# The SSD opening of a hybrid diffusion block: the positive part of the time steps on VectorE, the scan mask on GpSimd

## The chip, the cores and the metric

One core of a Trainium2 chip runs the whole program as one launch. The metric is device time in microseconds (us) of one execution. Of an engine's work the profile tells start and length of each instruction; the engines are TensorE (PE, with its weight loads as PEld), VectorE (DVE), ScalarE (ACT), GpSimd (POOL) and SyncE (SP), whose queue issues the DMAs. Each works through its own queue strictly in order and waits for the others by semaphores.

## The reference, cut to what matters

Two layers run over 512 latent tokens and 256 context tokens of width 1024. Layer 0 mixes tokens by attention, layer 1 by a bidirectional Mamba-2 state-space mixer (SSD); a gated feed-forward network with a short convolution follows each. What the edit touches is the front of the SSD mixer, in which a projection gives one time step for each token, head and direction:

```python
z, xbc, dt = jnp.split(h @ w_in, [D_INNER, D_INNER + CONV_DIM], axis=-1)
xbc = jax.nn.silu(dwconv_centred(xbc, conv_w, conv_b))
...
dt_f = jax.nn.softplus(dt_f.reshape(...) + dt_bias_f)
dt_b = jax.nn.softplus(dt_b.reshape(...) + dt_bias_b)
...
acs = jnp.cumsum(dtc * a, axis=2)          # within each chunk of 128 tokens
```

From `dt` and `acs` come all decays of the scan: `decay_end`, `chunk_decay`, and the matrix `exp(acs_q - acs_s)` of each chunk and head.

## The kernel before

Everything is float32. Each large matrix product is done as three matmuls on rounded halves (`mm3`, lines 108, 109 and 111: high weight by high activation, high by low, low by high), so every weight tile that SP loads (`wst`) is cast on ACT to its high half `wh` and split on DVE into its low half `wl` (lines 85 and 87). The buffers of these weight tiles rotate through ten places, so that the load, the cast and the split of a tile wait for a product some products earlier.

The program is written in the order of the mathematics; a scheduler of the framework then orders the instructions of each engine by a cost model of its own, so that an edit at one place can change the order at others. Buffers rotate by tags: of the PSUM tag `S` (two banks each, two of them) the projection tiles `ps_first` and `ps_in` take the slot that comes free first.

The SSD stage goes like this. `first_tiles` makes the first two products while the norm's last columns are still being worked out: `ps_dt`, the time steps (64 rows twice: rows 0 to 63 for tokens 0 to 383, rows 64 to 127 for tokens 384 to 767), and `ps_x0`, the first x tile; in the profile both are called `ps_first`. From `ps_dt` the time steps are made as softplus(v) = max(v, 0) + ln(1 + exp(-|v|)): `dte` holds |v| and its exponential, `dt` the positive part, `dtu`, `dtd` and `dtl` the logarithm with a correction; then `la` = dt times a (in `dte`), and `acs` by four scans on DVE (32 rows each, two directions, two halves), which multiply the running sum by a mask `msk` that is 0 at the first token of each chunk and 1 elsewhere.

Meanwhile `inproj(0)` makes the products of head group 0 in the order x, x, B, C, z, z. ACT copies each from PSUM to one of two buffers `raw`, multiplies by the middle tap (line 1063), DVE adds four taps (line 1065), ACT applies Silu (line 1069). When the first z tile is under way, `acs` and `dt` are transposed on TensorE (`ps_dtT`), copied to `acsT` and `dtT`, and `ps_end` spreads each chunk's last sum to all rows. Then `core(0)` makes decays, states and outputs of the group, interleaved with the products of the next; after eight groups the output projection (`ps_wo`, lines 1285 and later) multiplies the gated outputs `hhy`/`hly` (tiles 0 to 7) and `yh`/`yl` (8 to 15).

Of the kernel before, what the change touches and what calls it, by code (L numbers as in the profile page):

```python
# [7 lines left out]
P = 128  # L8
F32 = mybir.dt.float32
F32R = mybir.dt.float32r  # L10
AF = mybir.ActivationFunctionType
ALU = mybir.AluOpType
# [55 lines left out]
def t3(g, name, dt=F32, n=T):  # L68
    return g.t3p.tile([P, n], dt, tag="t3", bufs=g.n3, name=name)
# [148 lines left out]
def follow(g, bi):  # L218

    if g.last_act is not None:  # L220
        g.tc.add_manual_dep(bi.ins, g.last_act.ins.name, mybir.DependencyInfo(
            mybir.DependencyClass.NoSync, mybir.DependencyReason.DATA), reason="order of tables")
    g.last_act = bi
# [757 lines left out]
def ssd(g, x, norm, wf, bg, close):  # L981


    nc, I, tc = g.nc, g.I, g.tc
    par = lambda name, j, rows=P: g.par[:rows, PC[name] + j : PC[name] + j + 1]
# [13 lines left out]
    t2 = lambda nm, dt=F32, n=512: g.t3p.tile([P, n], dt, tag="t2", bufs=39, name=nm)  # L999
# [14 lines left out]
    TH = T // 2  # L1014
    r64 = lambda nm: t3(g, nm)[:, :TH]
    e, u, d0, dt = r64("dte"), r64("dtu"), r64("dtd"), r64("dt")
    for i in range(2):
        hs, src = slice(i * H2, (i + 1) * H2), ps[i * H2 : (i + 1) * H2, i * TH : (i + 1) * TH]
        nc.scalar.activation(e[hs], src, AF.Abs, bias=par("dtb", 0)[hs])
        nc.scalar.activation(dt[hs], src, AF.Relu, bias=par("dtb", 0)[hs])  # L1020
    follow(g, nc.scalar.activation(e, e, AF.Exp, scale=-1.0))

    nc.vector.tensor_scalar(u, e, 1.0, None, ALU.add)
# [6 lines left out]
    nc.vector.tensor_tensor(lnu, lnu, d0, ALU.add)  # L1030
    nc.vector.tensor_tensor(lnu, lnu, e, ALU.mult)
    nc.vector.tensor_tensor(dt, dt, lnu, ALU.add)
    la, acs, msk = e, r64("acs"), u
    nc.vector.tensor_scalar(la, dt, na, None, ALU.mult)
    nc.vector.memset(msk, 1.0)
    nc.vector.memset(msk.rearrange("p (c t) -> p c t", t=P)[:, :, 0:1], 0.0)

    for i in range(0, P, H2):
        f, b = slice(i, i + 32), slice(i + 32, i + 64)
# [185 lines left out]
    for gi in range(8):  # L1225
        i = -1
        for G in inproj(gi):
# [6 lines left out]
            if gi == 0 and i == 3:  # L1234
# [22 lines left out]
                for d in range(2):  # L1257
                    hs = slice(d * 32, d * 32 + 32)
# [4 lines left out]
                for d, t in enumerate((4, 5)):  # L1263
                    hs = slice(d * 32, d * 32 + 32)
# [92 lines left out]
def body(nc, tc, I, out, dbg=None):  # L1357
# [75 lines left out]
    def close():  # L1433
        phf.close()
        phx.close()

    x, nrm, first = ssd(g, x, nxt, wf, bg, close)
    phf = ExitStack()
    g.t3p, g.n3 = pool("pg", phf), 24
# [103 lines left out]
```

## Time and profile before

| | us |
|---|---|
| median of 3 runs | 1867.41 |
| lowest and highest | 1865.88 and 1868.11 |
| the profiled execution | 1865.96 |
| its span, first to last instruction | 1864.2 |
| PE busy | 1841.1 |
| DVE busy | 1305.0 |
| ACT busy | 809.6 |
| POOL busy | 304.3 |

The opening of the SSD stage lies at about 965 to 1010 us of the span, its output projection at about 1390 to 1490. In the rows of the timeline shown below stand start, length, engine, line, operation, what it writes and reads, and in brackets the idle time of the engine before it and what ended that.

### The profile page before, as it was taken

The numbers are of one execution on the slowest core, as the hardware profiler recorded it, in microseconds if no ns is written. First come the engines' busy times: TensorE is split into PE (matmuls) and PEld (weight loads), VectorE is DVE, ScalarE is ACT, GpSimd is POOL, SyncE is SP. The second block draws the span as 40 slices with busy tenths as digits, with TensorE's granted clock in tenths as the row PEclk, the third lists the DMA queues.
The fourth block names the chain that finished last, engine by engine and source line by source line (L and its number), as shares of the span: only waits on it lengthen the run. The fifth ranks groups of instructions, "written<-read, shape, count | busy, mean of one in ns | idle before, by whom it ended". The sixth has DMA issues, their size and how long they took to land.

```text
span 1864.2 us, 28839 instructions
## 1 busy us (share of the span) xinstructions
PE 1841.1 (99%) x11474; PEld 1542.8 (83%) x11474; DVE 1305.0 (70%) x1972; ACT 809.6 (43%) x1424; POOL 304.3 (16%) x266
## 2 busy tenths in 40 slices
PE   9999999999999999999999999999999999999999
PEld 8875655798888888888988888888888888888887
DVE  6588888778787776554487787777797575565655
ACT  4544434363222212222367667776666352323231
POOL 2123120040000000000032334444443210000000
PEclk9999999999999999999999999999999999999999
DMA  9233141124444552211224432433453223223232
GB/s 347 76 109 110 62 171 52 57 81 171 146 136 135 198 187 102 68 59 55 69 91 142 125 105 89 125 125 113 125 177 95 74 97 101 92 95 98 91 103 89
DMA packets 74070, 211.67 MB, mean 114 GB/s; under 512 B 9040, under 2 KB 14544, under 8 KB 73808
## 3 DMA queue, kind: packets, MB, share of 16 engines
q1 hardware_dynamic: 73936, 209.84, 34.2%
q8 instruction: 90, 1.47, 0.3%
q14 instruction: 44, 0.36, 0.1%
HBM read 198.79 MB, written 6.82 MB: 110 GB/s over the span
## 4 chain that ended last, share of the span: by engine, by line
PE 84%; DVE 7%; issue 3%; ACT 2%; POOL 2%; DMA 2%; SPq 0%; DVEq 0%; POOLq 0%; ACTq 0%
PE ps_up L111 10%; PE ps_up L109 10%; PE ps_up L108 10%; PE ps_d L108 7%; PE ps_d L109 6%; PE ps_d L111 6%; PE ps_in L111 4%; PE ps_in L109 4%; PE ps_in L108 4%; PE ps_s L700 2%; PE ps_o L664 2%; PE ps_st L1135 2%; PE ps_wo L111 1%; PE ps_wo L108 1%; PE ps_wo L109 1%
## 5 line engine op out<-in xcount | busy, mean ns | idle before, releaser
L87 DVE TENSOR_TENSOR wl<-wst,wh 128x1024 fp32r<-128x1024 f32 x207 | 258.0, 1246 | 221.4 <-PE ps_up L109 125.4
L85 ACT CAST wh<-wst 128x1024 fp32r<-128x1024 f32 x211 | 221.2, 1049 | 342.3 <-DMA wst<-in_wup 272.4
L111 PE MATMUL ps_up<-hhf,wl 128*128 128x512 f32 x1008 | 355.8, 353 | 0.0
L109 PE MATMUL ps_up<-hlf,wh 128*128 128x512 f32 x1008 | 355.8, 353 | 0.0
L108 PE MATMUL ps_up<-hhf,wh 128*128 128x512 f32 x1008 | 355.7, 353 | 0.0
L111 PEld LDWEIGHTS ps_up<-hhf,wl 128*128 128x128 f32 x1008 | 190.7, 189 | 25.9
L109 PEld LDWEIGHTS ps_up<-hlf,wh 128*128 128x128 f32 x1008 | 189.2, 188 | 25.9
L108 PEld LDWEIGHTS ps_up<-hhf,wh 128*128 128x128 f32 x1008 | 189.1, 188 | 25.8
L108 PE MATMUL ps_in<-hhs,wh 128*128 128x512 f32 (+1 forms) x560 | 203.7, 364 | 1.5 <-ACT dt L1020 1.5
L109 PE MATMUL ps_in<-hls,wh 128*128 128x512 f32 (+1 forms) x560 | 198.7, 355 | 0.0
L111 PE MATMUL ps_in<-hhs,wl 128*128 128x512 f32 (+1 forms) x560 | 198.2, 354 | 0.0
L108 PE MATMUL ps_d<-hdh,wh 128*128 128x512 f32 (+1 forms) x568 | 193.2, 342 | 0.3 <-ACT hdh L85 0.2
L109 PE MATMUL ps_d<-hdl,wh 128*128 128x512 f32 (+1 forms) x568 | 193.3, 341 | 0.0
L111 PE MATMUL ps_d<-hdh,wl 128*128 128x512 f32 (+1 forms) x568 | 193.1, 340 | 0.0
L877 DVE SCALAR_TENSOR_TENSOR X<-ps_d,mod,X 128x512 f32<-128x512 f32 (+1 forms) x224 | 125.1, 586 | 34.6 <-PE ps_d L111 34.0
L108 PEld LDWEIGHTS ps_in<-hhs,wh 128*128 128x128 f32 x560 | 105.5, 188 | 16.5 <-ACT dt L1020 1.7
L109 PEld LDWEIGHTS ps_d<-hdl,wh 128*128 128x128 f32 x568 | 106.9, 188 | 13.3 <-DVE hdl L87 0.4
L111 PEld LDWEIGHTS ps_d<-hdh,wl 128*128 128x128 f32 x568 | 107.6, 189 | 12.2
L111 PEld LDWEIGHTS ps_in<-hhs,wl 128*128 128x128 f32 x560 | 105.2, 188 | 14.8
L108 PEld LDWEIGHTS ps_d<-hdh,wh 128*128 128x128 f32 x568 | 106.4, 188 | 13.2 <-ACT hdh L85 0.7
L109 PEld LDWEIGHTS ps_in<-hls,wh 128*128 128x128 f32 x560 | 105.3, 188 | 13.4
L703 ACT ACTIVATE pr<-ps_s 128x1024 f32<-128x1024 f32 x56 | 57.2, 1022 | 104.6 <-PE ps_s L702 104.6
(339 smaller groups left out, 3661.2 us busy)
## 6 DMA issues: line engine op xcount, KB each, us to landing
wst<-in_wup SPq DMA_DIRECT2D x88, 512.0 KB, 3.3
wada<-in_adaT SPq DMA_DIRECT2D x56, 512.0 KB, 3.3
wst<-in_win SPq DMA_DIRECT2D x48, 512.0 KB, 3.4
wst<-in_wdown SPq DMA_DIRECT2D x44, 512.0 KB, 3.8
E<-ad SPq DMA_DIRECT2D x64, 256.0 KB, 6.4
wada<-in_adaB SPq DMA_DIRECT2D x24, 512.0 KB, 4.1
ec<-ead SPq DMA_DIRECT2D x64, 128.0 KB, 5.0
wst<-in_wout SPq DMA_DIRECT2D x16, 512.0 KB, 3.3
```

The costliest lines, as they stand in the source:

```text
L85: cast = keep(nc.scalar.copy(hi, src))
L87: keep(eng.tensor_tensor(lo, src, _r(hi), ALU.subtract))
L108: mm(out, wh, ah, start=first, stop=False)
L109: mm(out, wh, al, start=False, stop=False)
L111: mm(out, wl, ah, start=False, stop=last)
L664: nc.tensor.matmul(po[S64[e], :n], v, pr[:, 512 * e + off : 512 * e + off + n], start=first, stop=last)
L700: nc.tensor.matmul(outs[e], kk[e][a][S64[e], k], b[S64[e], q], start=i == 0, stop=False)
L703: exps.append(nc.scalar.activation(pr, ps, AF.Exp))
L877: nc.vector.scalar_tensor_tensor(ap, o[:, c0:c1], gate[:, m, v : v + 1], ap, ALU.mult, ALU.add)
L1135: nc.tensor.matmul(ps[:, d * 256 : (d + 1) * 256], Bt[:, t * P : (t + 1) * P], xw[d][t], start=t == ts[0], stop=t == ts[-1])
```

## The change

The Relu of each half, which ACT did behind the Abs of the same half, becomes one DVE instruction (add the bias, then maximum with 0) that reads the same half of `ps_dt` out of PSUM. The mask gets a buffer of its own from the tag `t2` (39 of them) instead of reusing `dtu`, and its two memsets move from DVE, between the steps of the logarithm, to POOL, with nothing ahead of them to wait for but their buffer.

```diff
@@ -1014,10 +1014,13 @@
     e, u, d0, dt = r64("dte"), r64("dtu"), r64("dtd"), r64("dt")
+    msk = t2("msk")[:, :TH]
+    nc.gpsimd.memset(msk, 1.0)
+    nc.gpsimd.memset(msk.rearrange("p (c t) -> p c t", t=P)[:, :, 0:1], 0.0)
     for i in range(2):
         hs, src = slice(i * H2, (i + 1) * H2), ps[i * H2 : (i + 1) * H2, i * TH : (i + 1) * TH]
         nc.scalar.activation(e[hs], src, AF.Abs, bias=par("dtb", 0)[hs])
-        nc.scalar.activation(dt[hs], src, AF.Relu, bias=par("dtb", 0)[hs])
+        nc.vector.tensor_scalar(dt[hs], src, par("dtb", 0)[hs], 0.0, ALU.add, ALU.max)
     follow(g, nc.scalar.activation(e, e, AF.Exp, scale=-1.0))
@@ -1030,10 +1033,8 @@
-    la, acs, msk = e, r64("acs"), u
+    la, acs = e, r64("acs")
     nc.vector.tensor_scalar(la, dt, na, None, ALU.mult)
-    nc.vector.memset(msk, 1.0)
-    nc.vector.memset(msk.rearrange("p (c t) -> p c t", t=P)[:, :, 0:1], 0.0)
```

The scheduler answers with another order at three places. (Line numbers of the changed kernel are three higher in the chain of `dt`, one higher from the scans on.) On ScalarE, from the first Abs on, there stood before:

```order
L1019 ACTIVATE dte<-ps_first,par 64x384
L1020 ACTIVATE dt<-ps_first,par 64x384
L1019 ACTIVATE dte<-ps_first,par 64x384
L1020 ACTIVATE dt<-ps_first,par 64x384
L1021 ACTIVATE dte<-dte 128x384
L1060 COPY raw_9692<-ps_first 128x512
L1026 ACTIVATE dtl<-dtu 128x384
L1062 COPY raw_9692<-ps_first 128x256
L85 CAST wh<-wst 128x1024 x2
L1063 ACTIVATE xf<-raw_9692,par 128x770
```

and now:

```order
L1022 ACTIVATE dte<-ps_first,par 64x384
L1061 COPY raw_9693<-ps_first 128x512
L1063 COPY raw_9693<-ps_first 128x256
L1022 ACTIVATE dte<-ps_first,par 64x384
L85 CAST wh<-wst 128x1024
L1024 ACTIVATE dte<-dte 128x384
L1029 ACTIVATE dtl<-dtu 128x384
L85 CAST wh<-wst 128x1024
L1061 COPY raw_9694<-ps_in 128x512
L1063 COPY raw_9694<-ps_in 128x256
L85 CAST wh<-wst 128x1024
```

The two copies of the first x tile (`raw`) moved between the two Abs, a weight cast moved ahead of the exponential, and a third cast ahead of the middle taps.

On VectorE, from the first tap of the first x tile, right behind the scans, there stood before:

```order
L1065 SCALAR_TENSOR_TENSOR xf<-raw_9692,par,xf 128x770
L87 TENSOR_TENSOR wl<-wst,wh 128x1024
L1065 SCALAR_TENSOR_TENSOR xf<-raw_9692,par,xf 128x770
L1065 SCALAR_TENSOR_TENSOR xf<-raw_9693,par,xf 128x770
L1065 SCALAR_TENSOR_TENSOR xf<-raw_9692,par,xf 128x770
L1065 SCALAR_TENSOR_TENSOR xf<-raw_9693,par,xf 128x770
L1065 SCALAR_TENSOR_TENSOR xf<-raw_9692,par,xf 128x770
L1065 SCALAR_TENSOR_TENSOR xf<-raw_9693,par,xf 128x770
L87 TENSOR_TENSOR wl<-wst,wh 128x1024
L1065 SCALAR_TENSOR_TENSOR xf<-raw_9693,par,xf 128x770
L1065 SCALAR_TENSOR_TENSOR Bf<-raw_9692,par,Bf 128x770 x2
L1241 COPY acsT<-ps_dtT 128x3x2x64
```

and now:

```order
L1066 SCALAR_TENSOR_TENSOR xf<-raw_9693,par,xf 128x770
L1066 SCALAR_TENSOR_TENSOR xf<-raw_9694,par,xf 128x770
L1066 SCALAR_TENSOR_TENSOR xf<-raw_9693,par,xf 128x770
L1066 SCALAR_TENSOR_TENSOR xf<-raw_9694,par,xf 128x770
L1066 SCALAR_TENSOR_TENSOR xf<-raw_9693,par,xf 128x770
L1066 SCALAR_TENSOR_TENSOR xf<-raw_9694,par,xf 128x770
L1066 SCALAR_TENSOR_TENSOR xf<-raw_9693,par,xf 128x770
L1066 SCALAR_TENSOR_TENSOR xf<-raw_9694,par,xf 128x770
L87 TENSOR_TENSOR wl<-wst,wh 128x1024
L1242 COPY acsT<-ps_dtT 128x3x2x64
L1242 COPY dtT<-ps_dtT 128x3x2x64
```

The weight splits that stood among the taps are gone from there (one stands ahead of the whole chain of `dt` now, right behind the positive parts), the two x tiles alternate from the start, and the copies `acsT` and `dtT` moved ahead of B's taps.

On TensorE, in the output projection, from the last matmul of the eighth y tile (numbers are of buffers, all one higher in the changed program), there stood before:

```order
L111 MATMUL ps_wo_13901<-hhy7_14128,wl_14108 128x512
L108 MATMUL ps_wo_14162<-hhy0_13908,wh_14151 128x512
L109 MATMUL ps_wo_14162<-hly0_13909,wh_14151 128x512
L111 MATMUL ps_wo_14162<-hhy0_13908,wl_14152 128x512
L108 MATMUL ps_wo_14162<-hhy1_13924,wh_14151 128x512
L109 MATMUL ps_wo_14162<-hly1_13925,wh_14151 128x512
```

and now:

```order
L111 MATMUL ps_wo_13902<-hhy7_14129,wl_14109 128x512
L108 MATMUL ps_wo_13901<-yh_14188,wh_14146 128x512
L109 MATMUL ps_wo_13901<-yl_14189,wh_14146 128x512
L111 MATMUL ps_wo_13901<-yh_14188,wl_14147 128x512
L108 MATMUL ps_wo_13901<-yh_14188,wh_14146 128x512
```

The first half of column block 4 (`hhy0` into a `ps_wo` of its own) gave its place to the ninth y tile (`yh`, `yl`), and follows most of it.

## The prediction

> **What bounds the kernel now.** I read the page's busy times and its chain first, then the busy time of stretches around the opening of the state-space (SSD) stage, then who TensorE waits for, then that opening in order of time.
>
> ```profile
> span 1864.2 us, 28839 instructions
> ...
> PE 1841.1 (99%) x11474; PEld 1542.8 (83%) x11474; DVE 1305.0 (70%) x1972; ACT 809.6 (43%) x1424; POOL 304.3 (16%) x266
> ...
> PE 84%; DVE 7%; issue 3%; ACT 2%; POOL 2%; DMA 2%; SPq 0%; DVEq 0%; POOLq 0%; ACTq 0%
> ```
>
> TensorE (PE) is busy for 1841.1 of 1864.2 us, at full granted clock; all its idle time in the kernel is about 23 us. A change on VectorE (DVE), ScalarE (ACT) or GpSimd (POOL) counts only where it lengthens or shortens a wait of TensorE.
>
> ```profile
> 955.00:1011.00 56.00, 52.03 (x312) 45.72 (x313) 47.10 (x77) 36.82 (x69) 4.50 (x6) 1.00 0.29 88
> 1011.00:1411.00 400.00, 397.33 (x2362) 343.35 (x2360) 305.63 (x345) 284.82 (x628) 170.43 (x145) 1.00 0.40 125
> ```
>
> The columns are the length of the stretch and the busy time of PE, weight loads, DVE, ACT and POOL. In the 56 us around the edit PE idles for 4.0 us; in the 400 us of head groups that follow, for 2.7 us. So the most that the edit can win at its place is a few tenths of a per cent.
>
> ```profile
> PE ps_in L108 <- ACT dt L1020: 1.5, 1, 1.5
> ...
> PE ps_end L1246 <- DVE acsT L1241: 1.0, 1, 1.0
> ...
> PE ps_wo L111 <- DVE wl L87: 0.4, 1, 0.4
> ```
>
> These are the waits that the changed order touches (total, times, longest): TensorE's first matmul into `ps_in` waits 1.5 us for the second Relu, `ps_end` 1.0 us for `acsT`, and one matmul of the output projection 0.4 us for a weight's low half. I take 0.2% of the time, 3.7 us, as what a measurement of this kernel can tell from no change.
>
> **The change, part by part.** First the rows of TensorE, ScalarE and VectorE in the opening (start, length, and in brackets the idle time and what ended it).
>
> ```profile
> 967.25 0.28 PE L111 MATMUL ps_first<-hhs,wl 128*128 128x256 f32 x1
> ...
> 969.00 0.38 PE L108 MATMUL ps_in<-hhs,wh 128*128 128x256 f32 x1 [1.47 <-ACT dt L1020]
> ...
> 991.58 0.48 PE L108 MATMUL ps_in<-hhs,wh 128*128 128x512 f32 x1
> ...
> 993.98 0.92 PE L1246 MATMUL ps_end<-acsT,cst 128*128 128x192 f32 x4 [1.00 <-DVE acsT L1241]
> ```
>
> ```profile
> 966.85 0.58 ACT L1019 ACTIVATE dte<-ps_first,par 64x384 f32<-64x384 f32 x1 [0.73 <-PE ps_first L111]
> ...
> 967.33 0.56 ACT L1020 ACTIVATE dt<-ps_first,par 64x384 f32<-64x384 f32 x1
> ...
> 970.43 0.36 ACT L1062 COPY raw<-ps_first 128x256 f32<-128x256 f32 x1
> ...
> 970.68 2.21 ACT L85 CAST wh<-wst 128x1024 fp32r<-128x1024 f32 x2
> ...
> 977.50 0.59 ACT L1060 COPY raw<-ps_in 128x512 f32<-128x512 f32 x1 [3.68 <-PE ps_in L111]
> ...
> 977.98 0.38 ACT L1062 COPY raw<-ps_in 128x256 f32<-128x256 f32 x1
> ...
> 991.48 0.85 ACT L1069 ACTIVATE xf<-xf 128x770 f32<-128x770 f32 x1
> ...
> 992.24 1.03 ACT L85 CAST wh<-wst 128x1024 fp32r<-128x1024 f32 x1
> ```
>
> ```profile
> 969.53 0.36 DVE L1023 TENSOR_SCALAR dtu<-dte 128x384 f32<-128x384 f32 x1 [3.21 <-ACT dte L1021]
> ...
> 975.88 0.38 DVE L1035 MEMSET dtu<- 128x384 f32 x1
> ...
> 976.17 0.49 DVE L1031 TENSOR_TENSOR dtl<-dtl,dte 128x384 f32<-128x384 f32 x1
> ...
> 980.65 0.95 DVE L1041 TENSOR_TENSOR_SCAN acs<-dtu,dte 32x384 f32<-32x384 f32 x1
> ...
> 981.63 1.02 DVE L1065 SCALAR_TENSOR_TENSOR xf<-raw,par,xf 128x770 f32<-128x770 f32 x1
> ...
> 982.57 1.22 DVE L87 TENSOR_TENSOR wl<-wst,wh 128x1024 fp32r<-128x1024 f32 x1
> ...
> 983.71 5.67 DVE L1065 SCALAR_TENSOR_TENSOR xf<-raw,par,xf 128x770 f32<-128x770 f32 x6
> ...
> 989.29 1.22 DVE L87 TENSOR_TENSOR wl<-wst,wh 128x1024 fp32r<-128x1024 f32 x1
> ...
> 993.37 0.55 DVE L1241 COPY acsT<-ps_dtT 128x384 f32<-128x384 f32 x1
> ```
>
> *The first wait (term A).* Before, Abs and Relu of the two halves run in turn on ACT, about 0.48 us apart, and PE's slot in PSUM comes free with the last Relu: the matmul before it ends at 967.25 + 0.28 = 967.53, the next starts at 969.00, 1.47 idle. In the changed program ACT runs one Abs, then the two copies of the first x tile out of the other `ps_first`, then the second Abs; so that other tile is free first, and `ps_in` takes its slot and waits for the second copy alone. The first copy can start 0.03 after 967.53 (a later pair, at 977.50, starts so behind PE), the second 0.48 later (977.50 to 977.98), and ends 0.38 after that: 968.42, PE 0.04 later at 968.46. The wait falls from 1.47 to 0.93: A = -0.54 us.
>
> *The dt chain and the slot for z (term B).* Copy 128x256 frees ACT after 0.25 (970.43 to 970.68), so the second Abs starts at 968.29 and ends 0.58 later, at 968.87. The positive part on DVE has no row before. Bounds: the DVE copy of 128x384 out of PSUM, 0.55, from above, and the one-input DVE row 128x384 out of SBUF, 0.36, from below; I take 0.55, since its source is PSUM. It reads the same PSUM half as the Abs, and in the program waits for it: the second ends at 968.90 + 0.55 = 969.45. But the scheduler now puts a weight split ahead of the chain: ACT's cast starts 0.48 after the Abs, at 968.77, lasts 1.03 and ends at 969.80; DVE's subtraction holds DVE for 1.14 (982.57 to 983.71) from 969.84, and `dtu`, which began at 969.53, begins at 970.98: 1.45 late. It is a split that the chain of before had not ahead of it; the other one, after the reciprocal, stays. The mask's memset held the chain for 0.29 (975.88 to 976.17) and leaves it; the short second memset lay under a dependency and gives nothing. So the last scan starts 1.16 later than at 980.65 and the conv taps begin at 982.79 instead of 981.63. Now the taps of both x tiles alternate, with no split between: eight at 0.93 (six in 5.58 from 983.71 to 989.29), the eighth from 989.30 to 990.32. ACT does both Silus before it empties B's PSUM: the second Silu from 990.36, 0.75 later (991.48 to 992.24 is such a step) 991.11 the first copy, 991.59 the second, ended at 991.97. TensorE wants that slot for z at 991.58 - 0.54 = 991.04 and gets it at 992.00: a new wait, B = +0.96. Its ends: 0 if the chain is 1 us less late than I make it, and 2.1 if the relay costs as much again.
>
> *`ps_end` (term C).* `acsT` now stands right behind the last split, ahead of B's taps: split at 990.23, copy from 991.37 to 991.92. `ps_end` comes at about 992.5, after two matmuls of z. The wait of 1.00 goes: C = -1.00 (ends: -1.00 and 0).
>
> *What follows.* Sum so far -0.58.
>
> ```profile
> 1000.61 0.82 PE L1116 MATMUL ps_bt<-cst,Bf 128*128 128x128 f32 x6
> ...
> 1007.62 1.89 PE L1135 MATMUL ps_st<-xw,Bt 128*128 128x256 f32 x8
> ...
> 1005.58 3.03 DVE L1123 TENSOR_TENSOR xw<-xt,dw 128x512 f32<-128x512 f32 x4
> ```
>
> B's transposes would be due at about 1000.25 (1000.61 less 0.58, one matmul later in order); B's taps start 1.0 us later than TensorE's time allows for free, but end with their Silu at 1000.05 by the same steps, just in time. The state matmuls would be due at 1007.04; `xw`, behind `dw`, moves with the later Silu of C by 0.8 us to 1006.4, and its first product is done at about 1007.1. D = +0.1, ends 0 and 0.8.
>
> *The mask on GpSimd.* Two memsets, 128x384 and 128x3.
>
> ```profile
> 1009.48 0.76 POOL L1168 TENSOR_SCALAR_AFFINE_SELECT E<-E 128x512 f32<-128x512 f32 x1 [45.54 <-DMA E<-ad]
> ```
>
> POOL idles for 45.5 us there, from 963.94 on. The mask is wanted by the first scan, three scans of 0.98 before the last at 981.81, so at about 978.9, 15 us into that idle time. Were that cover gone, the memset would cost as DVE's did, 0.4 us, or POOL's 0.76 for 128x512. Cost 0. Nothing waits behind it: the next POOL work starts with a DMA. On SP's queue z's weight load now stands ahead of the `ad` store instead of behind it, and a later load behind the eight `E` loads instead of ahead. ACT's cast and DVE's split of a load lie between it and TensorE, and the stretch of 400 us shows hardly a wait; cost 0, ends 0 and 0.6 per group (a rival below).
>
> *The output projection (term E).* The scheduler's order changes here too, far from the edit: of the weight loads, one lies a step later, so TensorE does the ninth y tile (`yh`, `yl`) where it did the first half of column block 4.
>
> ```profile
> 1425.13 0.64 ACT L1216 ACTIVATE ysq<-z 128x512 f32<-128x512 f32 x1 [5.86 <-DVE z L1214]
> ...
> 1425.66 2.55 ACT L1285 ACTIVATE yh<-z,par 128x512 fp32r<-128x512 f32 x4
> ...
> 1419.62 0.74 DVE L1286 SCALAR_TENSOR_TENSOR hly<-z,par,hhy 128x512 fp32r<-128x512 f32 x1
> ...
> 1425.01 1.22 DVE L87 TENSOR_TENSOR wl<-wst,wh 128x1024 fp32r<-128x1024 f32 x1
> ...
> 1426.41 3.51 DVE L1286 SCALAR_TENSOR_TENSOR yl<-z,par,yh 128x512 fp32r<-128x512 f32 x4 [0.17 <-ACT yh L1285]
> ...
> 1425.28 0.39 PE L108 MATMUL ps_wo<-hhy,wh 128*128 128x512 f32 x1
> ...
> 1426.29 0.50 PE L111 MATMUL ps_wo<-hhy,wl 128*128 128x512 f32 x1 [0.39 <-DVE wl L87]
> ```
>
> At 1425.28 TensorE started `hhy0` of block 4 and waited 0.39 for its `wl`. Now it starts there with `yh`. ACT writes that only behind the square `ysq`, which waits for z: begun at 1425.66, about 0.7 long (2.55 for four), so the matmul starts at 1426.40, 1.12 late. `yl` follows on DVE from 1426.41, 0.74 long like the `hly` row: 1427.15; the second matmul, due at 1426.63, waits 0.55. The third needs the `wl` that ended at 1426.23. So 1.67 of waits take the place of 0.39: E = +1.3 (ends -0.4 and +2.5, if the next cast, behind four `yh`, is late too).
>
> **Sum.** A -0.54, B +0.96, C -1.00, D +0.1, E +1.3: +0.8 us. The profiled execution took 1865.96 us (span 1864.2 and 1.8 around it), 1.45 under the median of the runs shown, 1867.41 (1865.88 to 1868.11). So 1866.8 for an execution like that, and 1868.2 for a median: the same, within what can be told.
>
> *A rule that speaks against the edit.* The trace of before shows Abs and Relu on one engine only, 0.48 us apart. The Trainium skill, "PSUM — Partial Sum Buffer", section "PSUM bank collisions raise a hardware error", says that two engines may not touch one PSUM bank in one 32-partition quadrant at once, ScalarE reading with VectorE reading included, and that such reads must be kept apart by semaphores. By that rule the positive part cannot run beside the absolute value of its half, only after it; no run here shows it yet. The sum above already has the reads in turn; read as beside each other, the second would end at about 968.84 instead of 969.45, under the cast, and the sum would be the same.
>
> **The rivals.**
>
> *Slower: the slot for z comes much later.* Two weight casts and a split now stand between the Abs and the scans, and TensorE's slot for z waits behind both Silus. From 3.7 us in all it decides: B would have to be 3.9 and not 0.96, the dt chain 2.9 us later still than I make it, as by a weight that lands late under the first cast. Then 1867.4 + 3.8 = 1871.2 or more. Against it: the two casts of before (from 970.68) started without a wait for their loads. A share of this rival is a load behind the `E` loads that comes late in each of seven groups, 0.6 us each, 4.2 us: 1871.6. Against it, the 2.7 us of idle PE time in 400.
>
> *The gain without the price.* A and C come as worked out, B's slot is in time, and E's order costs no more than the 0.39 it replaces: 1867.4 - 1.5 = 1865.9. For it: B hangs on a chain of a dozen steps of which each is a few hundredths uncertain; against it, both waits follow from in-order queues.
>
> *The reads in turn hold the slot.* If TensorE's first `ps_in` waits for the second positive part after all, it starts at 969.49 and not 968.46, A = +0.49. But then z wants its slot at 992.07, just after it is free, and B = 0: sum +0.9, 1868.3, another way to the same time. For it: the relay between ACT and DVE; against it: the program's wait there is for ScalarE alone.
>
> *The edit does nothing.* Then 1867.4; its time cannot be told from the forecast.
>
> **How the numbers follow.** Forecast as summed, 0.60; gain without price 0.20; reads in turn 0.10; slower 0.08; and 0.02 for a gain over 3.7 us, for which all idle time of the 56 us would have to go. The first three and most of their bounds lie within 0.2% of 1867.41 (1863.7 to 1871.1): same 0.90, slower 0.08, faster 0.02. The range goes from the second rival's 1865.9 less 0.9 for the spread of runs to the forecast with D and E at their upper ends (+1.9) and 1.0 of spread: 1865.0 to 1871.1.
>
> **What would show it.** In the changed profile: the wait of `ps_in` down to about 0.9 and ended by ACT's copy; the first positive part on DVE right behind the first Abs; `dtu` at about 1.4 us later against PE; a wait of about 1 us at the first matmul of z; no wait at `ps_end`; a wait of about 1.1 for ACT and 0.5 for DVE at `yh` and `yl`. A wait of z over 2 us, or TensorE waits spread over the groups, would make it wrong.

## The result, and the profile after

In nine runs each, side by side, the changed kernel took 1872.17 us in the median (1870.56 to 1876.58) and the kernel before 1868.11 (1865.79 to 1871.56): ratio 1.0023, 95% interval 1.0015 to 1.0031. That is 4.1 us slower (2.8 to 5.8), where the forecast was the same time with an upper end of 1871.1.

The profiled execution of the changed kernel is its longest, 1876.58 us, and not all of that is the edit's: TensorE is already 5.46 us late at the first matmul of the SSD stage (945.74 against 940.28), ahead of everything that the edit touches, mostly through stretches at half clock: four of 3.4 us lie ahead of that mark, against two in the execution of before. (A fifth, from 1514.5, lies behind the last mark of the table.) So the table takes TensorE's own marks, the start of the first matmul into each tile, and counts from that mark.

| start of | before | after | later, beyond 5.46 | terms that bear on it |
|---|---|---|---|---|
| first `ps_in` | 969.00 | 973.92 | -0.54 | A |
| `ps_cb` | 1006.74 | 1011.91 | -0.29 | A, B, C |
| first `ps_st` | 1007.62 | 1014.31 | +1.23 | D |
| first `ps_wo` | 1393.14 | 1399.82 | +1.22 | head groups: nothing |
| next stage (`ps_first`) | 1494.91 | 1504.14 | +3.77 | E |

The page's span, and TensorE's waits in the opening and in the projection (total, times, longest):

```profile
span 1874.8 us, 28832 instructions
...
PE ps_in L108 <- ACT raw L1063: 2.0, 2, 1.0
...
PE ps_st L1136 <- DVE xw L1124: 1.3, 1, 1.3
...
PE ps_bt L1117 <- ACT Bf L1070: 0.2, 1, 0.2
...
PE ps_wo L109 <- DVE yl L1287: 1.0, 1, 1.0
...
PE ps_wo L108 <- ACT yh L1286: 0.5, 1, 0.5
PE ps_y L1210 <- DVE E L1185: 0.2, 1, 0.2
```

The wait at `ps_end` is gone, as is that of `ps_wo` for `wl`; `ps_in` waits twice instead of once; three waits are new, `ps_st`, `yh` and `yl`, and two short ones of 0.2, at `ps_bt` and at `ps_y` for VectorE's `E`. The opening in order of time, TensorE, ScalarE, VectorE and GpSimd:

```profile
973.92 0.39 PE L108 MATMUL ps_in<-hhs,wh 128*128 128x256 f32 x1 [0.95 <-ACT raw L1063]
...
997.80 0.50 PE L108 MATMUL ps_in<-hhs,wh 128*128 128x512 f32 x1 [1.04 <-ACT raw L1063]
...
998.37 0.81 PE L1247 MATMUL ps_end<-acsT,cst 128*128 128x192 f32 x4
```

```profile
972.29 0.58 ACT L1022 ACTIVATE dte<-ps_first,par 64x384 f32<-64x384 f32 x1 [0.74 <-PE ps_first L111]
...
973.49 0.38 ACT L1063 COPY raw<-ps_first 128x256 f32<-128x256 f32 x1
973.89 0.58 ACT L1022 ACTIVATE dte<-ps_first,par 64x384 f32<-64x384 f32 x1
974.49 1.05 ACT L85 CAST wh<-wst 128x1024 fp32r<-128x1024 f32 x1
...
972.90 0.61 DVE L1023 TENSOR_SCALAR dt<-ps_first,par 64x384 f32<-64x384 f32 x1 [1.14 <-ACT dte L1022]
974.50 0.62 DVE L1023 TENSOR_SCALAR dt<-ps_first,par 64x384 f32<-64x384 f32 x1 [0.99 <-ACT dte L1022]
975.58 1.23 DVE L87 TENSOR_TENSOR wl<-wst,wh 128x1024 fp32r<-128x1024 f32 x1 [0.45 <-ACT wh L85]
976.72 0.35 DVE L1026 TENSOR_SCALAR dtu<-dte 128x384 f32<-128x384 f32 x1
...
971.39 0.42 POOL L1018 MEMSET msk<- 128x384 f32 x1 [2.01 <-DVE hls L304]
```

Each positive part on VectorE starts 0.03 us behind the Abs of its half and takes 0.61, so the two readers of that PSUM half go in turn and not beside each other. The weight split of 1.23 stands between it and `dtu`, as the order said.

### The profile page after: what moved, and what is told of

The parts are those of the page before. It is cut to its first block, busy times and chain, and to the rows that moved or that the text cites. A ratio compares the mean times of both kernels' runs of the same rounds, so it can differ in the third digit from the quotient of the medians.

```text
span 1874.8 us, 28832 instructions
## 1 busy us (share of the span) xinstructions
PE 1846.7 (99%) x11474; PEld 1546.7 (83%) x11474; DVE 1311.6 (70%) x1972; ACT 808.1 (43%) x1422; POOL 302.1 (16%) x268
## 4 chain that ended last, share of the span: by engine, by line
PE 85%; DVE 7%; issue 3%; DMA 2%; ACT 2%; POOL 1%; SPq 0%; DVEq 0%; ACTq 0%; POOLq 0%
PE ps_up L108 10%; PE ps_up L111 10%; PE ps_up L109 10%; PE ps_d L108 7%; PE ps_d L109 6%; PE ps_d L111 6%; PE ps_in L109 4%; PE ps_in L111 4%; PE ps_in L108 4%; PE ps_s L700 2%; PE ps_o L664 2%; PE ps_st L1136 2%; PE ps_wo L109 1%; PE ps_wo L111 1%; PE ps_wo L108 1%
```

## The experiments

The theory after the first look: the edit's own steps (A, B, C) cost nothing in sum; the loss comes from orders that the scheduler changed with it, which put VectorE's work beside GpSimd's where TensorE waits for it. The rival: moving the positive part, or the mask, costs in itself, or the loss is spread and a matter of the clock. All ratios, and the differences of time, are to runs of the kernel before on the same chip.

**One part alone: `x_relu` and `x_mask`.** `x_relu` is the kernel before with this, and `x_mask` is the changed kernel without it:

```diff
-        nc.scalar.activation(dt[hs], src, AF.Relu, bias=par("dtb", 0)[hs])
+        nc.vector.tensor_scalar(dt[hs], src, par("dtb", 0)[hs], 0.0, ALU.add, ALU.max)
```

> Only the positive part moves to VectorE; the mask stays where it was, written by VectorE into dtu inside the dt chain. On TensorE, ScalarE and SyncE the order in the opening and at the output projection is that of the changed kernel. Theory (the loss is in the order that the moved positive part brings: E loads of the first head group earlier, y tiles of the projection earlier, both onto VectorE while GpSimd works): the whole loss stays, ps_in waits about 2.0 us in two times, the first state matmul waits over 1 us, the projection's yl about 1 us; time before + 3.5 to 4.5 us, ratio about 1.002. Rival (the mask on GpSimd or its buffer costs it): ratio within 1.0005 of 1.

> Only the mask moves (own buffer, GpSimd); Abs and Relu stay on ScalarE in turn. Order of the projection and of SyncE around the E loads as in the kernel before; the dt chain is 0.29 us shorter, ps_end stands two matmuls earlier in TensorE's order. Theory: first ps_in wait 1.5 as before, ps_end wait 1.0 + 0.45 - 0.29 = about 1.2, no wait of about 1 at the projection's y tiles; time before + 0 to 0.5 us, ratio 1.0000 to 1.0004. Rival (mask costs): ratio about 1.002.

`x_relu`: 1870.31 us, ratio 1.0015 (1.0006 to 1.0024), 3.3 us more, with the waits of the changed kernel: `ps_in` 2.1 in two, `yl` 1.0, `yh` 0.5; `ps_st` only 0.6, where over 1 was expected. `x_mask`: 1868.21, ratio 1.0006 (0.9997 to 1.0014), with the waits of the kernel before in their place. So the waits say that the moved positive part, and not the mask, brings the loss; by time alone the two runs are not quite apart, since their intervals overlap (1.0006 to 1.0014). In `x_mask` one figure was missed: `ps_end`, two matmuls earlier in the order, waits 2.1 and not 1.2.

**Projection's order put back, `x_proj`.** Constraints on TensorE's order alone:

```diff
+            if k == 7:
+                first4.append(i)          # last matmul of block 4's first half
...
-                mm3(..., [(pm[i], ys[k])], k == 0, k == 15)
+                last = mm3(..., after=first4[0] if k in (8, 9) else None)
...
-    norm = rstd_rows(g, acc[0], L, ...)
+    norm = rstd_rows(g, acc[0], L, ..., after=last)
```

> The changed kernel with the output projection alone put back into the order of before (first half of column block 4 ahead of the ninth and tenth y tile, the norm's sums behind these). The opening is the changed kernel's, instruction for instruction. Theory: of the changed kernel's +3.8 us the 2.5 at the projection go: between the projection's start and the next stage TensorE is back at the time of before (101.8 us from 1393.14 to 1494.91), the ps_st wait of 1.3 stays; time before + 1.2, ratio about 1.0007. Rival (the loss is spread or a matter of clock, not of this order): time as the changed kernel, ratio 1.002.

It missed on the wrong side: 1875.02 us, ratio 1.0039 (1.0025 to 1.0053). Waits of `x_proj` in the projection:

```profile
PE ps_wo L108 <- ACT wh L85: 3.3, 1, 3.3
PE ps_wo L113 <- DVE wl L87: 1.2, 1, 1.2
```

With the old order TensorE waits 3.3 us for the high half and 1.2 for the low half of block 4's weight. The weight is late; drawing the y tiles forward was the cheaper way round this (the projection took 104.32 us so, and 108.59 here). That pointed to the queue of weight loads, ahead of the projection, which the runs on that queue below try.

**GpSimd's last addition left out, `x_noadd`.**

```diff
-            else:
+            elif (gi, pr) != (7, 1):
                 nc.gpsimd.tensor_tensor(acc[0], acc[0], sq, ALU.add)
```

> The changed kernel without GpSimd's last addition of squares (the tenth-last step of the norm: the sum lacks one tile of sixteen). Every other engine has the same order. Theory (VectorE's first yl takes 1.5 us instead of 0.75 because GpSimd adds squares beside it): first yl back at about 0.75 us, the four at 2.7 to 2.8 instead of 3.50, and TensorE's second y matmul starts 0.7 to 0.8 us sooner after the first (0.8 instead of 1.54). Rival (yl is late by ScalarE's yh or by VectorE's own queue): 1.54 stays.

The rows in the changed kernel (ScalarE, GpSimd, VectorE, TensorE), then in `x_noadd`:

```profile
1431.81 0.63 ACT L1217 ACTIVATE ysq<-z 128x512 f32<-128x512 f32 x1 [5.25 <-DVE z L1215]
1432.35 2.54 ACT L1286 ACTIVATE yh<-z,par 128x512 fp32r<-128x512 f32 x4
...
1432.58 1.46 POOL L1221 TENSOR_TENSOR ysq<-ysq 128x512 f32<-128x512 f32 x1 [2.26 <-ACT ysq L1217]
...
1433.09 3.50 DVE L1287 SCALAR_TENSOR_TENSOR yl<-z,par,yh 128x512 fp32r<-128x512 f32 x4 [0.18 <-ACT yh L1286]
...
1433.11 0.51 PE L108 MATMUL ps_wo<-yh,wh 128*128 128x512 f32 x1 [0.50 <-ACT yh L1286]
1434.65 0.50 PE L109 MATMUL ps_wo<-yl,wh 128*128 128x512 f32 x1 [1.04 <-DVE yl L1287]
```

```profile
1426.11 2.74 DVE L1287 SCALAR_TENSOR_TENSOR yl<-z,par,yh 128x512 fp32r<-128x512 f32 x4 [0.18 <-ACT yh L1286]
...
1426.13 0.50 PE L108 MATMUL ps_wo<-yh,wh 128*128 128x512 f32 x1 [0.50 <-ACT yh L1286]
1426.92 0.50 PE L109 MATMUL ps_wo<-yl,wh 128*128 128x512 f32 x1 [0.28 <-DVE yl L1287]
```

This kernel leaves one tile of sixteen out of the norm's sum and was run once, for the rows alone. Without the addition the four `yl` take 2.74 instead of 3.50, and the second matmul follows the first after 0.79 instead of 1.54: as the theory had it. The addition begins 0.5 us ahead of the first `yl` and is done at 1434.04; `yl` is ready 0.6 later, about its own length of 0.7.

**One place on SyncE's queue: `x_eload` and `x_before_eload`.** In the changed kernel the eight `E` loads of the first head group stand ahead of the weight load for C of the second group, in the kernel before behind it. SyncE's rows, changed kernel and before:

```profile
1005.73 5.66 SPq L1168 DMA_DIRECT2D E<-ad  x8
```

```profile
1005.26 5.60 SPq L1167 DMA_DIRECT2D E<-ad  x8
```

Counted from `ps_cb` (5.17 us later after) the loads are issued 4.7 us earlier. `x_eload` is the changed kernel with the old place forced, `x_before_eload` the kernel before with the new one:

```diff
 # x_eload
     d = g.nc.sync.dma_start(st, dram)
+    if before:
+        behind(g, before, d)      # before = first E load; d = weight load (group 1, C)
 # x_before_eload
+    if late:
+        behind(g, d, late)        # late = the eighth E load
```

> The changed kernel with one constraint more: on SyncE's queue the eight E loads of the first head group stand behind the weight load for C of the second group, as they did before. Up to the state matmuls TensorE, ScalarE and VectorE have the changed kernel's order; the output projection falls back into the order of before by itself. Theory (the loss hangs on this one place on SyncE's queue: E loads come about 4 us earlier, so GpSimd's selects run beside VectorE's dw and xw; and every later weight load comes a step later, so the projection does y tiles early): A, B, C as in the changed kernel, ps_st waits 0 to 0.6, dw back at 0.55, no waits for yh and yl; time before + 0 to 0.7 us, ratio 1.0000 to 1.0004. Rival (the moved positive part itself costs): ratio 1.002.

> The kernel before, without the edit, with the opposite constraint: that weight load stands behind the eight E loads. Abs, Relu and mask as before. The projection then takes the changed kernel's order by itself. Theory: without any part of the edit the larger part of the loss appears: no change at ps_in and ps_end, ps_st waits up to 0.5, at the projection the waits for yh (0.5) and yl (1.0) and 1.8 to 2.5 us in all; time before + 2 to 3 us, ratio 1.0011 to 1.0016. Rival: the load's place is nothing, ratio within 1.0004 of 1.

And the changed kernel beside them:

> The changed kernel again, unaltered, on the same chip as the three others, to compare them with. Both theories: before + 3 to 4.5 us, ratio 1.0016 to 1.0024.

| | load ahead of the E loads | load behind them |
|---|---|---|
| without the edit | before: 1 | `x_before_eload`: 1.0024 (1.0015 to 1.0033) |
| with the edit | `x_eload`: 1.0002 (0.9994 to 1.0011) | `x_same`: 1.0023 (1.0014 to 1.0032) |

The loss goes with the column, and nothing that can be told goes with the row: the kernel without any part of the edit becomes as slow by the place of one load (1869.73 us, more than was expected), and the edit without it costs nothing that can be told (1867.38, where before took 1866.51). The quotients of the medians are smaller than the ratios in the right column, 1.0017 and 1.0015, and larger in `x_eload`, 1.0005. Why the scheduler moves this load when the positive part moves was not traced. The waits in the projection follow, in `x_eload` as before, in `x_before_eload` as in the changed kernel:

```profile
PE ps_wo L113 <- DVE wl L87: 0.4, 1, 0.4
```

```profile
PE ps_wo L111 <- DVE yl L1289: 1.1, 1, 1.1
...
PE ps_wo L110 <- ACT yh L1288: 0.5, 1, 0.5
```

Every weight load behind that one comes a step later up to the projection, where the last group's load stands in the place that a projection weight had. In the opening the place decides what GpSimd does beside VectorE. Changed kernel, then `x_eload`:

```profile
1010.54 1.45 POOL L1169 TENSOR_SCALAR_AFFINE_SELECT E<-E 128x512 f32<-128x512 f32 x1 [38.57 <-DMA E<-ad]
1012.29 2.36 POOL L1169 TENSOR_SCALAR_AFFINE_SELECT E<-E 128x512 f32<-128x512 f32 x3 [0.31 <-DMA E<-ad]
...
1011.41 0.98 DVE L1262 TENSOR_TENSOR dw<-dw,dtT 128x384 f32<-128x384 f32 x1
1012.43 0.65 DVE L1266 TENSOR_TENSOR dw<-dw,dec 128x32 f32<-128x32 f32 x2
1013.00 3.93 DVE L1124 TENSOR_TENSOR xw<-xt,dw 128x512 f32<-128x512 f32 x4
```

```profile
1009.04 0.86 POOL L1172 TENSOR_SCALAR_AFFINE_SELECT E<-E 128x512 f32<-128x512 f32 x1 [44.06 <-DMA E<-ad]
...
1004.43 0.55 DVE L1265 TENSOR_TENSOR dw<-dw,dtT 128x384 f32<-128x384 f32 x1
1005.02 0.29 DVE L1269 TENSOR_TENSOR dw<-dw,dec 128x32 f32<-128x32 f32 x2
1005.24 3.03 DVE L1127 TENSOR_TENSOR xw<-xt,dw 128x512 f32<-128x512 f32 x4
```

Under the selects `dw` takes 0.98 instead of 0.55, its two small products 0.65 instead of 0.29, the four `xw` 3.93 instead of 3.03. In `x_same` `dw` began at 1004.40, in `x_eload` at 1004.43, and `ps_st` still waited 0.96 where `x_eload` waits 0.13 (1.18 from `ps_cb` less that row's 1.05): 0.83 us go with GpSimd's selects. The Trainium skill, "SBUF — State Buffer", section "Who interferes with whom", says that a VectorE instruction with two SBUF inputs contends with a GpSimd instruction that reads SBUF. The trace agrees in the rows of `yl`, `dw` and `xw`, all with two such inputs.

The load's place does not need both ends to cost that much. In `x_before_eload` the selects also lie beside `xw` (3.90), but `dw` keeps its 0.55 and TensorE goes from `ps_cb` to `ps_st` in 0.88, as before; the profiled loss lies in the projection, 103.68 us against 101.77, and 0.4 in the head groups. And in `x_eload` TensorE, counted as in the table above, is 0.60 ahead at `ps_st` and has lost that again at the first `ps_wo` (+0.02).

**The cast ahead of the dt chain, `x_chain`.**

```diff
-        ld = lambda i: load_w(g, I["win"][6 * gi + i])
+        ld = lambda i: load_w(g, I["win"][6 * gi + i], after=ln if gi == 0 and i in (2,) else None)
```

> The changed kernel with one weight cast of the opening held behind the chain's Ln on ScalarE, so that no weight split of VectorE stands ahead of the dt chain; E loads and projection in the changed kernel's order. Theory for term B (the new wait of z's first matmul is the price of the cast and split ahead of the chain): the second ps_in wait of 1.0 goes, dtu begins about 1.2 to 1.5 sooner against TensorE; the projection's 2.5 us stay; time before + 1.5 to 2.5 us, ratio 1.0008 to 1.0013. Rival (the wait of z comes from both Silus standing ahead of B's copies, whatever the chain): the wait of 1.0 stays, ratio 1.002.

1870.14 us, ratio 1.0016 (1.0008 to 1.0025). TensorE's waits in the opening:

```profile
PE ps_end L1248 <- DVE acsT L1243: 2.0, 1, 2.0
PE ps_in L108 <- DVE dt L1023: 1.2, 1, 1.2
```

Half right: the wait of z's first matmul is gone. But the run does not show that the split ahead of the chain was its price, since more came back with it: ScalarE copies B at 987.96, ahead of its second Silu at 989.76, and VectorE has `acsT` behind two of B's taps again (989.89 and 992.00). With that order `ps_end` waits 2.0, and the first `ps_in` 1.2, now for VectorE's positive part. So B and C hang together: what TensorE no longer waits for B's slot, it waits for `acsT`, all the more as that stands later here.

**A try at something faster, `x_fast`.** `x_eload`, and ScalarE's second Silu of the opening held behind the two copies that empty B's slot:

```diff
-            nc.scalar.copy(raw[:, L + 4 : L + 4 + C], ps[:, L:T])
+            c = nc.scalar.copy(raw[:, L + 4 : L + 4 + C], ps[:, L:T])
+            if raw_n[0] == 3:
+                behind(g, silus[1], c)
```

> The changed kernel with the E loads put back behind that weight load, and with ScalarE's second Silu of the opening held behind the two copies that empty B's PSUM slot. Theory: A and C stay (ps_in 0.95, no ps_end wait), B's wait of 1.0 goes, ps_st 0 to 0.6, projection as before; time before - 0.5 to - 1.5 us, ratio 0.9992 to 0.9998, which so many rounds hardly tell from 1. Rival (the wait only moves on, to the transposes of x, which wait for the later Silu): ratio 1.0000 to 1.0004.

1867.23 us, ratio 1.0001 (0.9991 to 1.0010): the rival's time. Its waits:

```profile
PE ps_in L110 <- ACT raw L1066: 0.9, 1, 0.9
PE ps_cb L1162 <- ACT Cf L1075: 0.9, 1, 0.9
PE ps_in L110 <- ACT z L1100: 0.6, 1, 0.6
```

B's wait is gone though the split still stands ahead of the chain (972.99, 1.23 long), so the Silu's place alone can remove it. Waits of 0.6 for z's slot, 0.9 at a later `ps_cb` and 0.3 at `ps_end` are there instead; the wait moved on, though not to the transposes of x. No version was found that beats the kernel before.

**The clock behind the waits, `x_same2` and `x_before_eload2`.** The same two kernels, one more execution each.

> The changed kernel once more, for the granted clock behind the projection's waits. Theory (waits of 0.5 and 1.0 within 2 us let TensorE's clock fall to half for one stretch of 3.4 us, but only in some executions): waits 0.5 and 1.0 as ever; a half-clock stretch at about 1428 to 1433 in two executions of three. Rival (the stretches fall anywhere): none there in most executions.

> The kernel before with the weight load behind the E loads once more, for the same question: waits of 0.5 and 1.0 at yh and yl, and a half-clock stretch right behind them in two executions of three; by the rival none there in most executions.

`x_same2` had the half-clock stretch (1428.2 to 1431.7), `x_before_eload2` had not; taken up in the last section.

## Why the prediction was wrong, step by step

The forecast summed to +0.8 us; TensorE's marks give +3.77. The 3.0 between them are 0.3 in A to C, 1.4 in D and 1.25 in E. (The forecast also stood on a median of 1867.41, where the kernel before took 1868.11 in the runs side by side.)

- **A, right.** -0.54 forecast, -0.54 measured: the slot comes free by the second copy (end 973.87), and the wait is 0.95 where 0.93 was worked out.
- **B and C, right here.** The new wait of z's first matmul is 1.04 (0.96 forecast), the one at `ps_end` is gone. Together with A they came to -0.29 and not -0.58 at `ps_cb`; 0.2 of that is the new wait at `ps_bt`, for which the forecast had B's Silu just in time. `x_chain` shows that B and C are not independent terms, as they were written: without B's wait, C's comes back at 2.0 (in `x_fast`, with `acsT` in its new place, at 0.3).
- **D, the size of one term.** +0.1 forecast; 1.5 came (+1.23 less -0.29). The term was mis-sized by the length of `dw` and `xw`, taken from rows in which GpSimd was idle. `x_eload`, in which it is idle again, waits 0.13: the working held without the overlap. Other executions with the changed kernel's opening wait 0.5 (`x_noadd`) to 1.4 (`x_proj`) at `ps_st`, so 1.5 is near the upper end of what the overlap costs. The forecast gave POOL's earlier start no thought, though the move of the `E` loads on SyncE's queue stood in its own text.
- **"On SP's queue ... cost 0", the step that failed.** The load behind the `E` loads was given 0, with 0.6 per group as an upper end, on the ground that the head groups hardly wait. They did not (385.52 us from `ps_st` to `ps_wo` before, 385.51 after). The load's place acts at the two ends of that stretch: through GpSimd's selects on D, and through the projection's late weight on E. `x_before_eload` shows it alone worth as much as the whole loss, there nearly all at the projection.
- **E, right place, wrong size.** +1.3 forecast, 2.55 measured. The start with `yh` came 0.5 late, less than the 1.12 worked out; `yl` 1.04, not 0.55, since its 0.74 was the row of an undisturbed `hly`. The row of four `yl` in 3.51 stood in the prediction beside it, 0.88 each against 0.74, and was not asked why: GpSimd's addition, 1.48 long from 1425.90, lay under that row too. These two waits less the 0.39 that they replace make about 1.2, and 0.2 is a wait of `ps_y` for VectorE's sum of E. The remaining 1.2 was not taken apart; 0.5 of it appears without the edit too, since `x_before_eload`, with the same waits, took 1.91 longer than before for its projection.
- **Reads of one PSUM half in turn, right.** The positive part follows each Abs by 0.03 us and takes 0.61 (0.55 assumed). It does so by a wait of the program's own, so the rule that the prediction quotes from the Trainium skill, "PSUM — Partial Sum Buffer", section "PSUM bank collisions raise a hardware error", was kept and not tried: no run here shows two such reads at once.
- **The rivals.** The slower one was given 0.08, with the right length (1871.2 or more) and a wrong mechanism for its greater part: z's slot came when it was due. Its smaller part, a load late behind the `E` loads, named the right instruction, but looked for its price in each group. Of the reads in turn that hold the slot there is nothing in the changed kernel, whose first `ps_in` is released by ScalarE's copy; in `x_chain`, where no copy stands between the two Abs, it did wait for the positive part.
- **Not in the sum at all:** a stretch at half clock, which the projection's new waits seem to draw in some executions (last section).

## What to carry to other kernels

When a change moves an order, follow the DMA queue first: here one load that slipped behind others shifted every load after it, and showed up 400 us later where a weight was wanted. Before a duration is taken from another row, look what GpSimd does beside it in the new place; a VectorE instruction with two inputs in SBUF took up to twice as long there (`dw` 0.98 against 0.55). And test a suspected order by itself, in both directions: with the edit and without it.

## What the hardware showed that was not expected

A wait of TensorE seems able to cost more than its length. The stretch of the projection, by windows of 3.5 us (length, busy time of TensorE with its matmuls, weight loads, VectorE, ScalarE, GpSimd, granted clock, DMA); `x_same`, then `x_before_eload`, with the same waits of 0.5 and 1.0 just ahead:

```profile
1424.00:1427.50 3.50, 1.94 (x8) 1.05 (x7) 3.33 (x4) 3.50 (x6) 1.46 (x1) 1.00 0.46 150
1427.50:1431.00 3.50, 3.50 (x10) 2.76 (x9) 3.50 (x6) 3.50 (x7) 0.00 (x0) 0.51 0.00 0
```

```profile
1431.00:1434.50 3.50, 3.50 (x17) 2.92 (x16) 3.50 (x5) 3.50 (x5) 0.00 (x0) 1.00 0.00 0
```

At a granted clock of 0.51, 10 matmuls are done in the time of 17. Of the eight profiled executions that had the waits for `yh` and `yl`, or for a late weight, at the projection, five show such a stretch of 3.41 us there (`x_relu`, `x_proj`, `x_chain`, `x_same`, `x_same2`), and three do not (the changed kernel's first, `x_before_eload` twice); of the five without those waits, or with 0.5 and 0.3 alone, none does. By its clock it is worth 1.7 us, half its length. The changed kernel's projection took 104.32 us without it and 105.92 with it in `x_same2` (105.02 in `x_same`, which lacks another wait of 0.9 there). At five of eight that is about 1.1 us in the mean, an estimate from these runs. That five fall so and none of the others speaks for the waits as the cause; no run lengthened a wait on purpose. Such stretches are not special to the projection: the execution of the kernel before has two, from 18.9 and from 278.3 (so its clock was nearly, not always, full, as the prediction has it), and three executions have one at about 1506 to 1518, the opening of the next stage, behind waits of 1.1 and 0.9 which every run has there. `x_mask` shows the same behind its wait of 2.1 at `ps_end`, in windows ahead of 994.0 and behind it:

```profile
990.00:994.00 4.00, 1.90 (x12) 1.41 (x11) 3.73 (x5) 3.16 (x5) 0.00 (x0) 1.00 0.29 110
994.00:997.40 3.40, 3.40 (x14) 3.02 (x13) 3.40 (x7) 2.13 (x4) 0.00 (x0) 0.50 0.00 0
```

The Trainium skill, "TensorE: Matmul & The Clock Gate", section "Part 1: The HAM clock gate (the "warmup" mystery)", says that the clock falls to half after an idle window of about 3.4 us, and that this window runs free of the kernel. The stretch's 3.41 us, and that it comes in some executions only, agree; but of the 3.41 us just ahead of these stretches TensorE's matmuls left only 1.5 to 1.6 us idle in `x_relu`, `x_chain`, `x_same` and `x_same2`, 2.1 in `x_mask` and 2.6 in `x_proj`, never a whole window, so the measurement decides: a window idle by about half can be enough. It is not always, since the changed kernel's first execution had the same waits without a stretch.
